# Two-layer hybrid attention trunk on one core: token loads first, the first conditioning in 128-column pieces, late outputs one step later

## The chip, the core and the metric

The kernel runs on one core of a Trainium2 chip. The metric is the device time of one execution in microseconds (us); lower is better. A core has the engines TensorE (PE, matrix products, with its weight loads shown apart as PEld), VectorE (DVE), ScalarE (ACT) and GpSimd (POOL), and SyncE (SP), which here issues transfers. POOL and ACT issue transfers too. All transfers of a core share 16 DMA engines.

## The reference, cut to what matters

128 context tokens (`x_prompt`) and 512 latent tokens (`x_sample`) of width 2048 go through two layers that share weights. Everything is float32.

```python
for layer in range(DEPTH):                       # DEPTH = 2
    sh_p, sc_p, gt_p = modulation(c_ctx, ada_w[layer], ada_b[layer])   # silu(cond) @ w + b, three parts of 2048
    sh_s, sc_s, gt_s = modulation(c, ada_w[layer], ada_b[layer])
    hp = rms_norm(xp, norm_g[layer]) * (1.0 + sc_p) + sh_p
    hs = rms_norm(xs, norm_g[layer]) * (1.0 + sc_s) + sh_s
    ...
        out_p, (kc, vc) = even_mixer(hp, *w)      # layer 0: windowed attention and short gated convolution
        out_s, _ = even_mixer(hs, *w, ctx=(cache_a_k[:, i], cache_a_v[:, i]), rope=rope)
    ...
        out_p, (ckc, cvc, dkc, dvc) = odd_mixer(hp, *w)   # layer 1: differential and grouped-query attention
    ...
    xp = xp + gt_p * out_p
    xs = xs + gt_s * out_s
```

`ada_w` is (2, 2048, 6144) float32. Its columns for one layer are 12 blocks of 512: blocks 0 to 3 give the shift, 4 to 7 the scale, 8 to 11 the gate. One block is 4.19 MB. A mixer starts with one wide projection of the 640 tokens, `h @ w_in`.

## The kernel before

**Layout.** Tokens stand in the free dimension: h is kept as 16 k-tiles (128 of the 2048 features by 640 tokens), each split into a high and a low part, and a weight tile `raw` (up to 4 k-tiles by 128 columns) is split into `wh` and `wl` by ACT and DVE (L241, L242). `proj_q` makes three products for each k-tile and each half of the tokens (320 wide, `pa` and `pb`): wh by high, wh by low, wl by high, at L276 to L278. In the text these are "main matmuls"; one k-tile of one column tile takes six.

**Start.** The conditioning vectors and small parameters are loaded as rows (`rows_a` by SP, `rows_b` by POOL), put through SiLU and transposed (L119 to L127). The tokens come as five blocks of 128 (`x_load`, two pieces of 512 KB each, the first two blocks through ACT's queue, the others through SP's). `x_block` transposes a block on PE in groups of four (L884), copies each group out of PSUM (L885) and sums the squares on ACT (L889); `x_rows` (L899) makes the per-token factor.

**Conditioning on PE.** `ada_on_pe(0, cb, h, n)` multiplies the condition with `n` times 128 columns of block `cb`: 16 small matmuls (L178; the profile shows two passes of each where the profile counts them), a copy, `n` transposes (L184), a reduction, the bias, and for scales the gain. The weights come by SP into two buffers of 2 MB used in turn (`ada_t`), and for block 5 into eight freed token buffers (`spare`, tile name `adah`). The profile's tile `ada` is the first kind.

**Lead phase of layer 0.** h is not there yet when projection starts, so `run_tiles` walks over k first: six column tiles ("leads", four of them summed in SBUF, `sum`) advance together through units of k-tiles. The units before are k 0 to 1, 2 to 3, then 4 to 7, 8 to 11, 12 to 13, 14 to 15 (argument `cut`). Before a unit `h0_maker` makes its h from shift and scale, and `ada_group` (through `ahead`) puts the conditioning of the next unit inside the current one. With four k-tiles to a group, unit 4 to 7 needs blocks 5 and 1. The six weight tiles of a unit are loaded by POOL into four `raw` buffers, except those of the first unit's first four, which SP loads. The order of instructions on each engine is set by a planner of the framework from the order of the code, and is the same in every execution.

**Odd layer.** While PE projects, generators in `attn` (attention) and `prep` (what follows a projected tile) are advanced in slots, four to a column tile; `steps` says how many attention steps a slot gives. `diff_gen` runs one head of the differential attention: scores, softmax, weighting (`weigh`), and `out`, which transposes the weighted result (L1391). The list `brisk` sets 1.1 steps to a slot from job 13 on. In `project_out` a finished output tile is added to the residual (`res_sum`, L1120) and for the second layer transposed to rows and written (`rows_out`, through `to_rows`, L564).

Of the kernel before, what the change touches and what calls it, by code (L numbers as in the profile page):

```python
# [11 lines left out]
F32 = mybir.dt.float32  # L12
# [8 lines left out]
P = 128  # L21
# [21 lines left out]
TRANS = [0, 3, 4, 5]  # L43
GRACE = 3
# [9 lines left out]
def trunk_kernel(ctx: ExitStack, tc: tile.TileContext, I: dict, O: dict):  # L54
# [36 lines left out]
    rows_a = wpool.tile([P, P], F32, tag="raw", name="rows_a")  # L91
# [9 lines left out]
    nc.sync.dma_start(rows_a[0:16, :], I["c"].rearrange("b (k p) -> (b k) p", p=P))  # L101
    nc.sync.dma_start(rows_a[16:32, :], I["c_ctx"].rearrange("(k p) -> k p", p=P))
    nc.sync.dma_start(ident, I["k_ident"])
    nc.sync.dma_start(rows_a[32:64, :], I["norm_g"].rearrange("l (k p) -> (l k) p", p=P))
    nc.sync.dma_start(rows_a[64:112, :], I["ada_b"][0].rearrange("(k p) -> k p", p=P))
    xs = [x_load(b) for b in range(5)]
    rows_b = wpool.tile([P, P], F32, tag="raw", name="rows_b")
# [3 lines left out]
    for i, n in enumerate(("a_q_norm", "c_q_norm", "d_q_norm")):  # L111
# [6 lines left out]
    th = wpool.tile([32, P], F32, tag="raw", name="th")  # L118
    A.activation(th, rows_a[0:32, :], AF.Tanh, scale=0.5)  # L119
    V.scalar_tensor_tensor(out=rows_a[0:32, :], in0=th, scalar=1.0, in1=rows_a[0:32, :],  # L120
                           op0=ALU.add, op1=ALU.mult)
    t0 = psT()
    PE.transpose(t0[:, 0:112], rows_a[0:112, :], ident[0:112, 0:112])
    PE.transpose(t0[:, 128:205], rows_b[0:77, :], ident[0:77, 0:77])
    V.tensor_scalar(sT[:, :, 0:2], t0[:, 0:32].rearrange("p (c k) -> p k c", c=2), 0.5, None, ALU.mult)
    V.tensor_copy(vec[:, 0:80], t0[:, 32:112])
    V.tensor_copy(vec[:, 80:157], t0[:, 128:205])  # L127
# [11 lines left out]
    def ada_done(l, cb, h=0, n=4):  # L139
        fs = slice(cb * 4 + 2 * h, cb * 4 + 2 * h + n)  # L140
        which, k0 = cb // 4, (cb % 4) * 4 + 2 * h
# [11 lines left out]
    def add_bias(l, cb, red, h=0, n=4):  # L153
        fs = slice(cb * 4 + 2 * h, cb * 4 + 2 * h + n)
        V.tensor_tensor(mod[l][:, fs, :], red, ada_b[l][:, fs][:, :, None].to_broadcast([P, n, 2]), op=ALU.add)

    def ada_on_pe(l, cb, h=0, n=4, spare=()):


        acc, m, wd = psT(), 2 if spare else 32 // n, n * P  # L160
        order, ws = list(range(KT)), []
        if spare:
            for i, s in enumerate(spare):
                w = hpool.tile([P, m, wd], F32, tag=f"h{s}", name="adah")
# [746 lines left out]
    for b in range(4):  # L911
        x_block(b, xs[b])
# [717 lines left out]
```

## Time and profile before

| what | value |
|---|---|
| time, median of 3 runs | 2301.63 us (2301.49 to 2303.0) |
| profiled execution | 2303.24 us, of which the span from first to last instruction is 2301.5 us |
| PE busy | 2255.1 us, 98% of the span |
| DVE, ACT, POOL busy | 73%, 43%, 8% of the span |
| mean granted PE clock | 0.997 |
| data moved | 347.52 MB, mean 151 GB/s |

A row of the time line reads: start, duration, engine, line, operation, tile written and tiles read, shape, count; in brackets the time that the engine was idle before it, and what it waited for. A row of the windows table gives for a stretch the busy time of each engine, the granted PE clock, the share of the DMA engines and the rate. Matmuls are pipelined: one of 0.31 us can follow another after 0.15 us.

### The profile page before, as it was taken

To read this page: it belongs to the slowest core of one execution; us is meant where nothing else is said; L and a number is where in the kernel's file an instruction comes from. 1 tells how busy PE (TensorE), PEld (TensorE's weight loads), DVE (VectorE), ACT (ScalarE), POOL (GpSimd) and SP (SyncE) were. 2 spreads that over 40 slices of the span, in tenths; PEclk is the share of its full clock that TensorE was granted. 3 is DMA by queue.
4 is the path that set the end of the run, shared out by engine and by line. 5 is a ranking of instruction groups with operands and counts; after the bars stand their busy time and mean duration, and the time that the engine had idled before them with its cause. 6 is when DMAs were issued, how large, how long until landed. Compare 5 with 4: busy or idle time off the path is not lost.

```text
span 2301.5 us, 41520 instructions
## 1 busy us (share of the span) xinstructions
PE 2255.1 (98%) x15796; PEld 2180.1 (95%) x15796; DVE 1676.7 (73%) x3364; ACT 991.3 (43%) x2043; POOL 182.6 (8%) x251
## 2 busy tenths in 40 slices
PE   7999999999999999999999999999999999999999
PEld 5699999999999999999999999999999999999999
DVE  4559886786877663888787765868868778677676
ACT  4235442433422222544654445455554554554343
POOL 2111000000000000000110000100000111111001
PEclk9999999999999999999999999999999999999999
DMA  9974535435355542954673334413324234237532
GB/s 367 332 257 127 163 117 171 141 113 174 106 179 175 155 140 82 296 150 134 212 240 115 112 119 144 136 58 93 112 74 145 75 114 132 78 106 240 167 120 70
DMA packets 389768, 347.52 MB, mean 151 GB/s; under 512 B 19330, under 2 KB 327056, under 8 KB 389056
## 3 DMA queue, kind: packets, MB, share of 16 engines
q1 hardware_dynamic: 376672, 296.32, 41.9%
q0 software_dynamic: 12176, 46.39, 5.3%
q8 instruction: 124, 2.03, 0.4%
q10 hardware_dynamic: 720, 2.16, 0.3%
q14 instruction: 76, 0.62, 0.1%
HBM read 303.89 MB, written 40.90 MB: 150 GB/s over the span
## 4 chain that ended last, share of the span: by engine, by line
PE 87%; DVE 5%; DMA 3%; ACT 2%; issue 2%; POOL 1%; SPq 0%; POOLq 0%; ACTq 0%; DVEq 0%
PE pa L276 9%; PE pb L276 9%; PE pb L277 9%; PE pa L278 9%; PE pa L277 9%; PE pb L278 9%; PE pq L535 7%; PE pq L537 7%; PE pq L536 7%; PE T L732 2%; PE S L744 1%; PE T L178 1%; PE S L746 1%; PE S L745 1%; PE T L564 1%
## 5 line engine op out<-in xcount | busy, mean ns | idle before, releaser
L241 ACT ACTIVATE wh<-raw 128x512 fp32r<-128x512 f32 (+1 forms) x442 | 273.3, 619 | 664.3 <-PE pb L277 550.3
L276 PE MATMUL pa<-h,wh 128*128 128x320 f32 x1504 | 478.0, 318 | 5.1 <-ACT h L241 2.6
L242 DVE TENSOR_TENSOR wl<-raw,wh 128x512 fp32r<-128x512 f32 (+1 forms) x442 | 297.6, 674 | 238.5 <-ACT wh L241 220.8
L277 PE MATMUL pa<-h,wh 128*128 128x320 f32 x1504 | 467.6, 311 | 1.4 <-DVE h L242 1.4
L278 PE MATMUL pa<-h,wl 128*128 128x320 f32 x1504 | 467.3, 311 | 0.0
L276 PE MATMUL pb<-h,wh 128*128 128x320 f32 x1504 | 466.1, 310 | 0.4 <-DVE xr L1120 0.4
L278 PE MATMUL pb<-h,wl 128*128 128x320 f32 x1504 | 466.3, 310 | 0.0
L277 PE MATMUL pb<-h,wh 128*128 128x320 f32 x1504 | 465.7, 310 | 0.0
L213 DVE SCALAR_TENSOR_TENSOR acc<-adaw,sT,acc 128x512 f32<-128x512 f32 (+1 forms) x600 | 360.3, 639 | 14.3 <-DMA adaw<-in_ada_w 13.8
L276 PEld LDWEIGHTS pa<-h,wh 128*128 128x128 f32 x1504 | 283.3, 189 | 17.6 <-issue 8.9
L277 PEld LDWEIGHTS pa<-h,wh 128*128 128x128 f32 x1504 | 284.1, 189 | 4.5 <-DVE h L242 2.2
L278 PEld LDWEIGHTS pa<-h,wl 128*128 128x128 f32 x1504 | 283.4, 188 | 3.7 <-issue 3.7
L278 PEld LDWEIGHTS pb<-h,wl 128*128 128x128 f32 x1504 | 282.8, 188 | 2.1 <-issue 2.1
L276 PEld LDWEIGHTS pb<-h,wh 128*128 128x128 f32 x1504 | 282.9, 188 | 0.6 <-issue 0.6
L277 PEld LDWEIGHTS pb<-h,wh 128*128 128x128 f32 x1504 | 282.9, 188 | 0.5 <-issue 0.4
L535 PE MATMUL pq<-h,wh 128*128 128x320 f32 x608 | 189.8, 312 | 0.5 <-ACT wh L241 0.5
L536 PE MATMUL pq<-h,wh 128*128 128x320 f32 x608 | 187.9, 309 | 0.0
L537 PE MATMUL pq<-h,wl 128*128 128x320 f32 x608 | 187.7, 309 | 0.0
L718 ACT ACTIVATE p<-S,nm,rq 128x768 f32<-128x768 f32 (+3 forms) x120 | 101.3, 844 | 101.7 <-DVE nm L713 70.1
L535 PE MATMUL pq<-T,wh 128*128 128x320 f32 x456 | 140.9, 309 | 0.0
L536 PE MATMUL pq<-T,wh 128*128 128x320 f32 x456 | 140.9, 309 | 0.0
L537 PE MATMUL pq<-T,wl 128*128 128x320 f32 x456 | 140.9, 309 | 0.0
(339 smaller groups left out, 3933.5 us busy)
## 6 DMA issues: line engine op xcount, KB each, us to landing
adaw<-in_ada_w SPq DMA_DIRECT2D x192, 256.0 KB, 2.9
raw<-in_ev_w_in SPq DMA_DIRECT2D x184, 256.0 KB, 3.0
raw<-in_od_w_in SPq DMA_DIRECT2D x160, 256.0 KB, 2.9
ada<-in_ada_w SPq DMA_DIRECT2D x14, 2048.0 KB, 10.1
adaw<-in_ada_w SPq DMA_DIRECT2D x128, 128.0 KB, 2.1
w<-in_od_w_in SPq DMA_DIRECT2D x24, 512.0 KB, 3.7
yd<-y POOLq DMA_DIRECT2D x32, 320.0 KB, 3.3
w<-yd SPq DMA_DIRECT2D x32, 320.0 KB, 4.1
```

The source lines that it names most:

```text
L178: PE.matmul(acc[32 * g:32 * g + 32, 0:wd], sT[:, kt, :], w[:, kt % m, :], start=(i < 4), stop=(i >= KT - 4), tile_position=(0, 32 * g))
L213: V.scalar_tensor_tensor(out=a, in0=w, scalar=sT[:, kt, c:c + 1], in1=a, op0=ALU.mult, op1=ALU.add)
L241: A.activation(hi, x, AF.Copy)
L242: V.tensor_sub(lo, x, hi)
L276: PE.matmul(ps, wh[:, i, :], hi[:, sl], start=(j == js[0] if alone else (pos == 0 and j == 0)), stop=False)
L277: PE.matmul(ps, wh[:, i, :], lo[:, sl], start=False, stop=False)
L278: PE.matmul(ps, wl[:, i, :], hi[:, sl], start=False, stop=(j == js[1] - 1 if alone else (pos == 3 and j == 3)))
L535: PE.matmul(ps, wh[:, j, :], hi, start=(h == 0 and j == 0), stop=False)
L536: PE.matmul(ps, wh[:, j, :], lo, start=False, stop=False)
L537: PE.matmul(ps, wl[:, j, :], hi, start=False, stop=(h == 1 and j == 3))
L718: A.activation(p[:, 0:n], s, AF.Exp, scale=rsc, bias=nm, accum_out=l)
L732: PE.transpose(t[:, i * P:(i + 1) * P], p, ident)
```

## The change

The five row loads of the conditioning go from SP's queue to POOL's, behind nothing but each other; SP's queue then begins with the identity and the tokens. Token blocks are loaded and transposed in the order 0, 2, 1, 3, 4, and the SiLU of the conditions and its transposes (`cond_in`) come after the fourth of them. `rows_a`, `rows_b` and `th` get places of their own instead of `raw` buffers. ACT copies the last group of a block only for even blocks; DVE copies it for the others.

The first halves of blocks 4 and 0 come as four loads of 128 columns (1 MB each), and the first unit of the lead phase is split in two, k 0 and k 1, so that there are seven units. Four of the eight pieces of block 5 are loaded ahead of the second halves of blocks 4 and 0.

In the odd layer `out` of a head's last block comes one step later, a finished output tile of the last projection is written one slot later, and `brisk` is 1.2 instead of 1.1.

```diff
+ORDER_X = (0, 2, 1, 3, 4)
+SPARE = (15, 14, 11, 10, 13, 12, 9, 8)
-    nc.sync.dma_start(rows_a[0:16, :], I["c"].rearrange("b (k p) -> (b k) p", p=P))
-    nc.sync.dma_start(rows_a[16:32, :], I["c_ctx"].rearrange("(k p) -> k p", p=P))
     nc.sync.dma_start(ident, I["k_ident"])
...
-    xs = [x_load(b) for b in range(5)]
+    xs = {b: x_load(b) for b in ORDER_X}
+    nc.gpsimd.dma_start(rows_a[0:16, :], I["c"].rearrange("b (k p) -> (b k) p", p=P))
...
+    def first_load(cb, j):
+
+        if cb not in first_ws:
+            first_ws[cb] = ada_t[0].rearrange("p (k n) -> p k n", k=KT)
+            ada_t.reverse()
+        c0 = cb * 512 + j * P
+        nc.sync.dma_start(first_ws[cb][:, :, j * P:(j + 1) * P],
+                          I["ada_w"][0, :, c0:c0 + P].rearrange("(k p) n -> p k n", p=P))
...
-            (A.copy if g == 3 else V.tensor_copy)(xT[g][:, :, b * P:(b + 1) * P],
+            (A.copy if g == 3 and b % 2 == 0 else V.tensor_copy)(xT[g][:, :, b * P:(b + 1) * P],
...
-    for b in range(4):
+    for i, b in enumerate(ORDER_X):
         x_block(b, xs[b])
-    ada_on_pe(0, 4, 0, 2)
-    x_block(4, xs[4])
+        if i == 3:
+            cond_in()
+    first_load(4, 0)
+    ada_on_pe(0, 4, 0, 1)
...
-        g = {(4, 0): 0, (4, 4): 1, (5, 0): 2, (5, 4): 3}.get((ui, n))
+        g = {(5, 0): 0, (5, 4): 1, (6, 0): 2, (6, 4): 3}.get((ui, n))
...
+    def first_ada():
+        for cb, j in ((0, 0), (4, 1), (0, 1)):
+            first_load(cb, j)
+        ada_on_pe(0, 0, 0, 1)
+
+        spare_load(0, 5, SPARE[:4])
...
-    run_tiles(jobs, I["ev_w_in"][0], h0_maker, fill0, FILL0, ada_group, trans=TRANS, grace=GRACE, cut=((0, 2), (2, 4)),
-              summed=keep, led=even_start, lead_in=lambda: ada_on_pe(0, 0, 0, 2))
+    run_tiles(jobs, I["ev_w_in"][0], h0_maker, fill0, FILL0, ada_group, trans=TRANS, grace=GRACE, cut={0: ((0, 1), (1, 2), (2, 4)), 3: ((0, 2), (2, 4))},
+              summed=keep, led=even_start, lead_in=first_ada)
...
                     res_sum(l, n, pp[i], CS[:1] if i == 0 else CS[1:])
                 yield
+                if l:
+                    yield
                 finish(n)
...
-            if u < 6:
-                yield
+            yield
             if u >= 2:
                 out(u - 2)
...
-    brisk.update((i, 1.1) for i in range(13, len(jobs)))
+    brisk.update((i, 1.2) for i in range(13, len(jobs)))
```

Two places show how the planner's order moves.

The first is SP's queue at the start. `ada` are pieces of blocks 4, 0 and so on in the two 2 MB buffers, `adah` the pieces of block 5, `raw` weight tiles of the projection. Before, then with the change:

```order
L101 DMA rows_a<-in_c 16x128
L102 DMA rows_a<-in_c_ctx 16x128
L103 DMA ident<-in_k_ident 128x128
L104 DMA rows_a<-in_norm_g 32x128
L105 DMA rows_a<-in_ada_b 48x128
L97 DMA xb<-in_x_sample 128x1024 x4
L97 DMA xb<-in_x_prompt 128x1024 x2
L175 DMA ada_120<-in_ada_w 128x16x256
L254 DMA raw<-in_ev_w_in 128x2x128 x4
L175 DMA ada_121<-in_ada_w 128x16x256
L175 DMA ada_120<-in_ada_w 128x16x256
L175 DMA ada_121<-in_ada_w 128x16x256
L165 DMA adah<-in_ada_w 128x2x512 x8
```

```order
L104 DMA ident<-in_k_ident 128x128
L100 DMA xb<-in_x_sample 128x1024 x4
L100 DMA xb<-in_x_prompt 128x1024 x2
L177 DMA ada_121<-in_ada_w 128x16x128
L277 DMA raw<-in_ev_w_in 128x128 x4
L177 DMA ada_122<-in_ada_w 128x16x128
L177 DMA ada_121<-in_ada_w 128x16x128
L177 DMA ada_122<-in_ada_w 128x16x128
L166 DMA adah<-in_ada_w 128x2x512 x4
L198 DMA ada_121<-in_ada_w 128x16x256
L198 DMA ada_122<-in_ada_w 128x16x256
L166 DMA adah<-in_ada_w 128x2x512 x4
```

The row loads are gone from this queue, two loads of 256 columns have become four of 128, and four pieces of block 5 stand ahead of the last two 256-column loads.

The second is PE around the conditioning of the first group of k-tiles (k 0 to 3, 144 main matmuls) and the start of the second (k 4 to 7). `T<-ada... 32x512 x8` is half of a block, `T<-ident,ada_sb` the transposes behind it, `pa<-h_896` (with the change `pa<-h_995`) the first main matmul of k 4. Before, the end of the first group:

```order
L276 MATMUL pb<-h_694,wh 128x320
L277 MATMUL pb<-h_694,wh 128x320
L278 MATMUL pb<-h_694,wl 128x320
L178 MATMUL T<-ada_121,sT 32x512 x8
L184 MATMUL T<-ident,ada_sb 128x128 x4
L276 MATMUL pa<-h_896,wh 128x320 x2
```

With the change, first the place after 72 main matmuls (k 0 and 1 done), then the place after 123:

```order
L301 MATMUL pb<-h_648,wl 128x320
L201 MATMUL T<-ada_121,sT 32x256 x16
L207 MATMUL T<-ident,ada_sb 128x128 x2
L201 MATMUL T<-ada_122,sT 32x256 x16
L207 MATMUL T<-ident,ada_sb 128x128 x2
L299 MATMUL pa<-h_794,wh 128x320 x2
```

```order
L301 MATMUL pa<-h_794,wl 128x320
L201 MATMUL T<-ada_122,sT 32x512 x8
L299 MATMUL pa<-h_801,wh 128x320
L300 MATMUL pa<-h_801,wh 128x320
L301 MATMUL pa<-h_801,wl 128x320
L299 MATMUL pb<-h_794,wh 128x320
L300 MATMUL pb<-h_794,wh 128x320
L207 MATMUL T<-ident,ada_sb 128x128 x4
```

The last half of block 1 stood behind all 144 main matmuls of the first group; with the change it stands behind 123, and 21 main matmuls lie between it and the second group. The second halves of blocks 4 and 0, which stood among main matmuls, now stand together after the first 72 with none between them and the h that needs them. Behind the lead phase the order on PE is the same up to the middle of the odd layer.

69 lines of the change are left out of this document (38 added, 31 removed).

## The prediction

> **What bounds the kernel now.** I read the page's totals first, then the time line of PE and the windows at the start, then what PE waited for in the odd layer.
>
> ```profile
> span 2301.5 us, 41520 instructions
> PE 2255.1 (98%) x15796; PEld 2180.1 (95%) x15796; DVE 1676.7 (73%) x3364; ACT 991.3 (43%) x2043; POOL 182.6 (8%) x251
> PE   7999999999999999999999999999999999999999
> ```
>
> PE is the bound; it lacks 2301.5 − 2255.1 = 46.4 us over the whole span. Of the 40 slices of the span only the first is below nine tenths busy. The change removes no main matmul, so it can win only idle time and time at a low clock. Here is the start on PE:
>
> ```profile
> 7.86 0.42 PE L123 MATMUL T<-ident,rows_a 112*128 112x112 f32 x1 [7.86 <-DMA rows_a<-in_ada_b]
> 10.93 4.40 PE L884 MATMUL T<-ident,xb 128*128 128x128 f32 x20
> 16.88 4.85 PE L884 MATMUL T<-ident,xb 128*128 128x128 f32 x24 [1.54 <-ACT xT L885]
> 32.91 1.93 PE L178 MATMUL T<-ada,sT 128*32 128x256 f32 x32 [0.45 <-ACT tables L900]
> 37.04 0.56 PE L276 MATMUL pa<-h,wh 128*128 128x320 f32 x2 [1.22 <-ACT h L926]
> 44.21 0.31 PE L276 MATMUL pb<-h,wh 128*128 128x320 f32 x1
> 47.43 0.31 PE L278 MATMUL Sp<-h,wl 128*128 128x320 f32 x1
> 60.88 3.64 PE L178 MATMUL T<-adah,sT 128*32 128x512 f32 x32
> 67.15 1.92 PE L178 MATMUL T<-ada,sT 128*32 128x512 f32 x16
> 71.10 1.92 PE L178 MATMUL T<-ada,sT 128*32 128x512 f32 x16
> 73.78 0.66 PE L184 MATMUL T<-ident,ada_sb 128*128 128x128 f32 x4 [0.76 <-ACT ada_sb L181]
> 75.68 0.90 PE L276 MATMUL pa<-h,wh 128*128 128x320 f32 x2 [1.24 <-ACT h L926]
> ```
>
> ```profile
> 39.00:41.00 2.00, 2.00 (x9) 1.80 (x7) 0.00 (x0) 0.45 (x2) 0.00 (x0) 0.50 1.07 375
> 77.00:79.00 2.00, 2.00 (x9) 2.00 (x8) 2.00 (x5) 0.70 (x2) 0.00 (x0) 0.50 1.03 407
> ```
>
> Two gaps are to be seen: before the first main matmul (37.04) and before the second group of k-tiles (75.68), where the last half of block 1 (71.10) must pass its copy, transposes, bias and h, 0.76 + 1.24 us of idle. The two rows of the windows (the granted clock is the number before the DMA share) show that after each of them PE ran at 0.50 of its clock. The 23 main matmuls from 44.21 to 47.43 come (47.43 − 44.21)/22 = 0.146 us apart. In a stretch of about 3.4 us at half clock, some 1.7 us of work is lost, an estimate from the 0.50 and from the spread of the slow rows between 75.68 and 79.
>
> What stands behind PE there is the transfer of weights:
>
> ```profile
> 0.00:5.00 5.00, 0.00 (x0) 0.00 (x0) 0.59 (x3) 0.00 (x0) 3.39 (x10) 1.00 0.53 179
> 5.00:10.00 5.00, 0.42 (x1) 0.18 (x1) 0.28 (x1) 3.78 (x6) 0.00 (x0) 1.00 0.99 321
> 10.00:20.00 10.00, 7.56 (x37) 5.79 (x37) 5.33 (x15) 5.50 (x11) 1.61 (x3) 0.88 1.03 401
> 20.00:25.00 5.00, 4.55 (x28) 3.08 (x27) 3.88 (x8) 4.56 (x9) 0.61 (x2) 0.90 1.11 373
> 25.00:30.00 5.00, 4.12 (x50) 2.57 (x48) 3.71 (x12) 2.62 (x8) 3.46 (x5) 1.00 1.09 385
> 30.00:45.00 15.00, 12.51 (x113) 9.20 (x111) 6.09 (x17) 5.48 (x13) 0.77 (x2) 0.89 1.07 381
> 45.00:50.00 5.00, 5.00 (x54) 3.88 (x53) 2.47 (x6) 1.55 (x5) 1.44 (x2) 1.00 1.04 397
> 50.00:65.00 15.00, 15.00 (x108) 11.82 (x107) 6.96 (x16) 6.32 (x16) 4.49 (x6) 1.00 1.04 406
> 65.00:70.00 5.00, 5.00 (x40) 3.33 (x39) 4.00 (x11) 1.35 (x3) 0.75 (x1) 1.00 0.73 261
> ```
>
> The DMA engines are full (share above 1) from 10 to 65 us. Multiplying rate by time gives the bytes moved: 2.5 MB at 10 us, 16.0 at 45, 18.0 at 50, 24.1 at 65. So until the second group starts, time is set by bytes as much as by PE.
>
> **The change part by part, the start.** The six-column lead phase needs, up to the last half of block 1: tokens 5.24 MB, small loads 0.14, four blocks of 4.19 (16.8), weight tiles of the first group 6 × 262 KB = 1.6, and the first four tiles of the second group 1.0; in all 24.8 MB. On the table that is 24.1 at 65 us and 0.7 more at 406 GB/s: 66.7 us. The change moves none of these bytes away; the early start of PE (transposes no longer behind the 7.86 us wait for the rows and the ACT copy at 16.88) is therefore worth only what the transfers allow.
>
> What changes in the transfers: SP's queue starts with tokens instead of five small loads. The first 10 us moved 2.5 MB where 401 GB/s would give 4.0; I take 1.0 us of this as won (bounds 0 and 1.5/0.401 = 3.7, the whole hole). The four 128-column loads read 512-byte rows instead of 1 KB. The trace has no window of such rows alone; the 20 to 25 window, with 0.52 MB of them (four tiles of 128 KB), ran at 373 against 381 to 385 around it: 1.34 MB at 0.383 takes 3.5 us, which leaves 1.5 us for 0.52 MB, 350 GB/s. For 4.19 MB that is 12.0 − 10.9 = 1.1 us lost (bounds 0, and 2.6 at 310 GB/s, twice the drop). The two cancel nearly. The Trainium skill, "DMA: Bandwidth & Descriptors", section Specifications, gives 512 bytes as the smallest transfer for line rate; by that the 1.1 us would be nothing and the sum below 1.1 us better.
>
> Now PE. In the new order four pieces of block 5 (2.1 MB) come ahead of the second halves of blocks 4 and 0. The half of block 0 is complete when 5.4 + 8.4 + 2.1 + 1.0 (weight tiles of k 0, 1 and the first of k 2) = 16.9 MB are in, 47.3 us on the table. PE is long through k 0 and 1: main work can begin near 28 us (tokens by about 16.5 us, 20 groups of four transposes at 4.85/6 = 0.8 us each from about 6 us, then two conditioning steps of about 3 us), and 72 × 0.146 = 10.5 us, half blocks 2 × 1.5 and a slow stretch end by 43 to 45. The matmuls of that half start at 47.5, and its chain is that from 32.91 to 37.04, 4.1 us, with a slow clock behind it: k 2 starts at 51.6. From there to the last half of block 1 lie 51 main matmuls (7.4), block 5 (3.64 and 0.45 for transposes), the first half of block 1 (1.92) and the slow clock (1.7): 66.8 us, the same moment as its bytes. I take 68 us for it, since the 261 GB/s row shows the queue running thin with that piece still on its way (bounds 65.5, and 70.5 with the dearer rows). Then 1.92 + 0.45 for its matmuls and transposes and 21 × 0.146 = 3.1 for the main matmuls that now follow it: 73.5 us, and the second group goes on at full clock, its h being made under those 21. Before, the same point was at 75.68 with 1.7 us of slow clock still to pay, in effect 77.4. **The start gains 3.9 us** (bounds: 1.4 with 70.5, and 7 with 65.5 and no slow clock). Behind it PE is the bound again, so the gain stays: no slice after the first is below nine tenths, and 10,692 instructions follow in unchanged order.
>
> ```profile
> L349 DVE TENSOR_TENSOR sum<-sum,pb 128x320 f32<-128x320 f32 x13 | 6.3, 487 | 5.3 <-PE pb L278 5.3
> ```
>
> What is costed at nothing: 32 more conditioning matmuls, at most the 1.93 us of a half block, run while PE waits for block 0; the additions of one more unit, 8 of 0.49 us, and shorter splits lie on DVE, busy 33 of these 70 us (sum of its column above); without that cover, 3.9 us. DVE's copies in blocks 1 and 3 instead of ACT's lie ahead of the first main matmul, where bytes decide. Rows on POOL's queue are ahead of everything that POOL issues; `cond_in`, fourth in line, waits for nothing else. The copies of x to DRAM shift by one unit number with the same matmuls.
>
> **The odd layer.** PE's waits there that the change touches:
>
> ```profile
> 1843.64 0.41 PE L1391 MATMUL T<-ident,on 128*128 128x128 f32 x2 [1.21 <-DVE on L1385]
> 1931.32 0.41 PE L1391 MATMUL T<-ident,on 128*128 128x128 f32 x2 [1.38 <-DVE on L1385]
> 2016.67 0.41 PE L1391 MATMUL T<-ident,on 128*128 128x128 f32 x2 [0.49 <-DVE mod L155]
> 2057.33 0.44 PE L1391 MATMUL T<-ident,on 128*128 128x128 f32 x2 [0.43 <-DVE ptl L242]
> 2124.83 0.41 PE L564 MATMUL T<-ident,xr 128*128 128x128 f32 x2 [0.31 <-issue]
> 2125.51 0.65 PE L564 MATMUL T<-ident,xr 128*128 128x128 f32 x3 [0.27 <-DVE xr L1120]
> 2154.17 0.93 PE L564 MATMUL T<-ident,xr 128*128 128x128 f32 x5 [1.06 <-ACT h L241]
> 1807.56 0.44 PE L744 MATMUL S<-k0h,q0h 128*128 128x384 f32 x1 [0.84 <-ACT p L718]
> 2077.72 0.39 PE L744 MATMUL S<-k1h,q1h 128*128 128x256 f32 x1 [1.07 <-ACT p L718]
> ```
>
> One more step for `out` and for the output tiles aims at 3.5 us (L1391) and 1.6 us (L564), 5.1 in all; some of it will show up at another place, since 16 of the 20 `out` calls are also moved by the new pace; I take 3.9. The pace of 1.2 for 15 jobs of 4 slots gives 60 × 0.1 = 6 more slots with two attention steps, of which 4 go to the four new steps. Two steps in a slot bring two scores close together; the two such waits in the stretch (0.84, 1.07) over its 6 double slots make 0.3 us for each, 1.9 us for six (bounds 0 and 6 × 1.07 = 6.4). **Net gain 2.0 us** (bounds −3.8, with half the gain and every double slot paid, and 5.1).
>
> Sum: 3.9 + 2.0 = 5.9 us from the profiled span, 2295.6. The profiled execution took 2303.24 us, 1.74 around its span, and so becomes 2297.3; it stands 1.6 above the median of the runs, which becomes 2301.63 − 5.9 = **2295.7 us**.
>
> **The rivals.** 0.2% (4.6 us) is about what a measurement of this kernel can tell from no change.
>
> *Bytes take it all.* The dearer rows and the pieces of block 5 in front make the last half of block 1 come at 70.5 or later: start 1.4, odd layer 1.5, time 2298.7. For: a full DMA from 10 to 65 us. Against: the hole before 10 us. Its sister, a price of 1 us for each new double slot, leaves the start's 3.9 and takes 2 to 4 back: 2299.7 to 2301.7.
>
> *The transfers give more.* The hole before 10 us is filled (3.7 us), the second group starts at 70.5 and the odd layer brings 4: 11 us, 2290.6. For: SP's queue held small loads only. Against: two queues already brought tokens from the start.
>
> *Weight tiles starve (slower).* With one k-tile to a unit, a weight tile feeds 6 × 0.146 = 0.88 us of PE, and four `raw` buffers are refilled by POOL:
>
> ```profile
> L254 POOL DMA_DIRECT2D raw<-in_ev_w_in x29: 705/722/779, 27.1 to 139.1; - x29
> DMA to landing us min/median/max: 2.5/5.7/11.5
> ```
>
> A turn of a buffer is 0.72 to issue, 5.7 to land and about 1 to split: 7.4/4 = 1.9 us for a tile, slower than 0.88 but covered by eight tiles loaded or split ahead and by the wait to 47.5. At 11.5 us it would be 13.2/4 = 3.3 us; then the six tiles of k 2 and 3 take 20 us instead of 10.5, the second group starts 9 us later than forecast, 82.7 against 77.4: 5.3 us lost, and 2307 without help from the odd layer. It decides from a turn of 4 × 1.75 = 7 us sustained, above which k 2 and 3 cannot be fed at PE's pace. For: more load in flight; against: the median.
>
> **How the numbers follow.** Forecast 0.47 (2293 to 2297); the transfers give more 0.13; bytes take it all 0.20 and its sister 0.09; starvation 0.11. The range from 2288.5 to 2302 holds the first four but for their tails, about 8 in 10. Faster 0.47 + 0.13 = 0.60, same 0.29, slower 0.11.
>
> **What would show it.** Right: the first main matmul near 28 us; after 72 main matmuls a gap of several us on PE that ends in h and is followed by half clock; no gap of 2 us and no half clock where the second group starts, and that start near 73.5; DMA share near 1 throughout; no wait over 1 us at the transposes of `out` for a head's last block, and some more waits of scores for the softmax. Wrong: the second group later than 76, or a gap inside k 2 and 3 that waits for `wh` or `raw`; forced attention steps in one slot before a new head's keys; more than 4 us of new waits for scores.

## The result and the profile after

The changed kernel took 2308.68 us (median of 8 runs, 2304.71 to 2311.37) where the kernel before took 2301.8 (8 runs, 2299.27 to 2304.27) on the same chip: ratio 1.0023, 95% interval 1.0013 to 1.0032. It is slower, by 5.3 us by the ratio and 6.9 us by the medians; 2295.7, faster, was predicted. Its profiled execution has a span of 2306.9 us, 5.4 more than before's.

First the time line of PE at the start of the changed kernel (start, duration, line, result and operands, and in brackets the idle time ahead and what ended it):

```profile
25.87 1.08 PE L201 MATMUL T<-ada,sT 128*32 128x128 f32 x32 [0.18 <-DVE ssx L915]
32.41 0.56 PE L299 MATMUL pa<-h,wh 128*128 128x320 f32 x2 [0.20 <-ACT h L951]
41.75 0.41 PE L299 MATMUL pb<-h,wh 128*128 128x320 f32 x1 [2.04 <-ACT sum L370]
50.23 0.39 PE L299 MATMUL pa<-h,wh 128*128 128x320 f32 x1 [3.24 <-DVE sum L372]
51.27 3.39 PE L201 MATMUL T<-ada,sT 128*32 128x256 f32 x32
55.50 1.93 PE L201 MATMUL T<-ada,sT 128*32 128x256 f32 x32
59.64 0.56 PE L299 MATMUL pa<-h,wh 128*128 128x320 f32 x2 [1.22 <-ACT h L951]
74.81 1.92 PE L201 MATMUL T<-ada,sT 128*32 128x512 f32 x16
80.34 0.66 PE L299 MATMUL pa<-h,wh 128*128 128x320 f32 x2
```

Then two rows of the windows table (busy us of PE, PEld, DVE, ACT and POOL, the granted clock, DMA share, GB/s):

```profile
52.00:54.00 2.00, 2.00 (x25) 0.92 (x20) 0.21 (x1) 0.00 (x0) 0.84 (x2) 0.50 1.07 418
74.00:82.00 8.00, 8.00 (x56) 5.69 (x55) 4.73 (x11) 4.18 (x8) 1.92 (x3) 1.00 1.04 399
```

The main matmuls start 4.6 us earlier (32.41 against 37.04). Then PE waits 2.04 and 3.24 us inside the first 72 of them, and from 51.27 to 59.64 there is no main matmul at all: the second halves of blocks 4 and 0 are conditioned one behind the other, the first at half clock (the 0.50 from 52 to 54 us). k 2 starts at 59.64 where it started at 54.13 before, and the second group at 80.34 where it was 75.68. At the second group the forecast picture stands: no gap, full clock from 74 to 82. So the change removed the gap it aimed at and made a longer one some 20 us ahead of it. At the 351st main matmul (123.98 us before, 127.90 after) the lag is 3.92 us.

Second, what the two waits are. ACT, which splits the weight tiles, waits for their transfers (same columns). What POOL's loads into the `raw` buffers take is in the view of that tile between 20 and 90 us:

```profile
41.07 0.31 ACT L264 ACTIVATE wh<-raw 128x128 fp32r<-128x128 f32 x1 [2.27 <-DMA raw<-in_ev_w_in]
47.23 0.42 ACT L264 ACTIVATE wh<-raw 128x256 fp32r<-128x256 f32 x1 [2.79 <-DMA raw<-in_ev_w_in]
48.81 0.42 ACT L264 ACTIVATE wh<-raw 128x256 fp32r<-128x256 f32 x1 [1.16 <-DMA raw<-in_ev_w_in]
```

```profile
L277 POOL DMA_DIRECT2D raw<-in_ev_w_in x22: 534/716/756, 23.9 to 82.6; - x22
DMA to landing us min/median/max: 3.9/5.1/6.4
```

PE names the copies `sum` of ACT and DVE as the releasers, but these stand in their engines' order behind a split that waits for a transfer (41.07 for the first wait, 48.81 for the second). It took no slow landing: 5.1 us is the median.

Third, what PE waited for in the odd layer, longest groups first (total, times, longest), before and after:

```profile
PE T L1391 <- DVE on L1385: 2.6, 2, 1.4
PE S L744 <- ACT p L718: 1.9, 2, 1.1
PE T L564 <- DVE m L620: 1.3, 4, 0.6
```

```profile
PE T L587 <- DVE m L643: 3.4, 5, 2.2
...
PE S L767 <- ACT p L741: 0.6, 2, 0.3
```

The waits for `on` are gone, and those for the softmax became smaller, not larger. In their place stands one of 2.2 us for `m`, the rotation of the first key of the second attention.

### The profile page after: what moved, and what is told of

It is laid out like the page before. It is cut to its first block, busy times and chain, and to the rows that moved or that the text cites. A ratio compares the mean times of both kernels' runs of the same rounds, so it can differ in the third digit from the quotient of the medians.

```text
span 2306.9 us, 41700 instructions
## 1 busy us (share of the span) xinstructions
PE 2263.4 (98%) x15860; PEld 2186.2 (95%) x15860; DVE 1682.7 (73%) x3385; ACT 988.7 (43%) x2049; POOL 184.2 (8%) x261
## 4 chain that ended last, share of the span: by engine, by line
PE 87%; DVE 4%; DMA 3%; issue 2%; ACT 2%; POOL 1%; SPq 0%; ACTq 0%; POOLq 0%; DVEq 0%
PE pa L299 9%; PE pb L299 9%; PE pb L300 9%; PE pb L301 8%; PE pa L300 8%; PE pa L301 8%; PE pq L558 7%; PE pq L560 7%; PE pq L559 7%; PE T L755 2%; PE S L767 1%; PE T L201 1%; PE S L769 1%; PE S L768 1%; PE T L587 1%
## 5 line engine op out<-in xcount | busy, mean ns | idle before, releaser
L264 ACT ACTIVATE wh<-raw 128x512 fp32r<-128x512 f32 (+2 forms) x448 | 274.5, 613 | 665.6 <-PE pb L300 544.2
L265 DVE TENSOR_TENSOR wl<-raw,wh 128x512 fp32r<-128x512 f32 (+2 forms) x448 | 298.7, 668 | 214.5 <-ACT wh L264 194.6
```

The costliest lines, as they stand in the source:

```text
L264: A.activation(hi, x, AF.Copy)
L265: V.tensor_sub(lo, x, hi)
```

## The experiments

Fifteen kernels were run. A ratio is the time over that of the kernel before, run beside it, with its 95% interval; 0.1% is 2.3 us. Each row of the table is one trace. The landings of the halves of blocks 4 and 0 are the end of the last packet of that half, counted by row length; that of the last half of block 1 is issue plus time to landing, because the next block's rows have its length. The three starts are those of the first, 73rd and 145th main matmul on PE's time line. Traces of kernels with the same lead phase scatter: the second group starts at 75.0 to 76.3 us with the start of before (four traces), at 73.1 to 74.5 with tokens first (four) and at 79.9 to 80.8 with the changed start (three).

| kernel | ratio, interval | first main | halves of blocks 4, 0 landed | k 2 | last half of block 1 landed | second group |
|---|---|---|---|---|---|---|
| before | 1 | 37.0 | 36.5, 42.8 | 54.1 | 69.1 | 75.7 |
| changed | 1.0023, 1.0013–1.0032 | 32.4 | 41.5, 48.8 | 59.6 | 69.6 | 80.3 |
| start alone | 1.0030, 1.0019–1.0040 | 33.2 | 42.7, 50.4 | 59.2 | 70.4 | 79.9 |
| weight tiles in own places | 1.0020, 1.0010–1.0030 | 32.8 | 44.0, 51.8 | 58.0 | 68.9 | 78.7 |
| no early pieces | 1.0039, 1.0027–1.0052 | 33.0 | 40.1, 47.7 | 56.9 | 72.9 | 80.1 |
| pieces between the halves | 1.0029, 1.0018–1.0040 | 32.4 | 40.7, 51.8 | 56.4 | 70.2 | 78.2 |
| the same, tiles in own places | 1.0037, 1.0023–1.0051 | 32.8 | 41.5, 51.1 | 57.8 | 68.5 | 81.0 |
| quarter in own place, no pieces | 1.0055, 1.0043–1.0068 | 32.3 | 36.7, 44.8 | 55.7 | 70.2 | 85.5 |
| the same, two k-tiles to a unit | 1.0030, 1.0019–1.0040 | 33.0 | 37.0, 43.6 | 51.7 | 70.2 | 80.0 |
| tokens first alone | 0.9996, 0.9987–1.0005 | 35.1 | 36.7, 43.4 | 50.7 | 69.9 | 74.5 |

**The three odd-layer edits alone.** The kernel before with

```
+                if l:
+                    yield
...
-            if u < 6:
-                yield
+            yield
...
-    brisk.update((i, 1.1) for i in range(13, len(jobs)))
+    brisk.update((i, 1.2) for i in range(13, len(jobs)))
```

> The kernel before with only the three odd-layer edits. Theory (the loss of the changed kernel sits in the lead phase, up to main matmul 350; the odd layer gives a little back): about 1 us faster than before, 2300.8 (2299.5 to 2302), no wait over 0.5 us at the transposes of out, start rows as before. My forecast's term says 2.0 us faster, 2299.8. Rival (the double slots of the pace cost more than the waits they remove, and this is why the changed kernel is slower): 2 to 4 us slower, 2304 to 2306, with several new waits of scores for the softmax.

Measured: 2305.14 against 2304.68, ratio 1.0000 (0.9991 to 1.0009): no change that can be told. The interval is 2.1 us to either side, so the rival's 2 to 4 us of loss are out but for their edge, and the theory's 1 us of gain is not decided. The waits of PE in the odd layer changed places:

```profile
PE T L564 <- DVE m L620: 5.3, 5, 3.5
```

No wait for `on` is left, and the one for `m` takes back 3.5 us. Its cause is on DVE's time line and in SP's queue. First the kernel before:

```profile
1767.19 0.69 DVE L600 TENSOR_TENSOR kg<-T,gain_rows 128x512 f32<-128x512 f32 x1 [0.83 <-ACT junk L598]
1768.95 0.48 DVE L213 SCALAR_TENSOR_TENSOR acc<-adaw,sT,acc 128x256 f32<-128x256 f32 x1 [0.79 <-DMA adaw<-in_ada_w]
```

```profile
1758.17 0.41 SPq L207 DMA_DIRECT2D adaw<-in_ada_w  x1
1763.24 0.82 SPq L1483 DMA_DIRECT2D y<-gd  x2
1764.63 2.08 SPq L207 DMA_DIRECT2D adaw<-in_ada_w  x3
```

Then this one:

```profile
1770.66 0.48 DVE L213 SCALAR_TENSOR_TENSOR acc<-adaw,sT,acc 128x256 f32<-128x256 f32 x1 [3.50 <-DMA adaw<-in_ada_w]
1771.06 0.68 DVE L600 TENSOR_TENSOR kg<-T,gain_rows 128x512 f32<-128x512 f32 x1
1776.50 0.68 DVE L620 TENSOR_TENSOR m<-m,m 128x512 f32<-128x512 f32 x1
```

```profile
1764.73 1.88 SPq L1484 DMA_DIRECT2D y<-gd  x2
1767.14 1.45 SPq L207 DMA_DIRECT2D adaw<-in_ada_w  x3
```

In both kernels three adaw loads stand behind the two gate copies `y<-gd`. Two things differ. Before, one more adaw load had gone out at 1758.17, ahead of the copies; now the next ones go out at 1767.14. And before, `kg` stood on DVE ahead of the step that waits for adaw; now this step, with its wait of 3.50 us, stands ahead of `kg` and so of `m`, which need no adaw, and PE stands behind `m`.

**The start alone.** The changed kernel with these three edits undone. The next seven kernels also have the odd layer of before.

> The changed kernel with the three odd-layer edits undone: its start alone. Theory: k 2 starts near 59.6 us and the second group near 80.3 as in the changed kernel, and the whole is 4 to 8 us slower than before, 2306 to 2310 (3.9 from the lead, and up to 3 where the transfers later meet a wait). Rival (the odd layer is the loss): the start alone is equal or faster, 2298 to 2302, whatever the lead phase shows.

Measured: 2311.07 against 2304.68, 1.0030 (1.0019 to 1.0040). The theory held, with k 2 at 59.2 and the second group at 79.9: the loss is in the start.

**Tokens first alone.** The start with block halves of 256 columns, two k-tiles to a unit and block 5 late, as before the change:

```
-    first_load(4, 0)
-    ada_on_pe(0, 4, 0, 1)
+    ada_on_pe(0, 4, 0, 2)
...
     def first_ada():
-        for cb, j in ((0, 0), (4, 1), (0, 1)):
-            first_load(cb, j)
-        ada_on_pe(0, 0, 0, 1)
-        spare_load(0, 5, SPARE[:4])
+        ada_on_pe(0, 0, 0, 2)
...
-    cut={0: ((0, 1), (1, 2), (2, 4)), 3: ((0, 2), (2, 4))}
+    cut={0: ((0, 2), (2, 4)), 3: ((0, 2), (2, 4))}
```

> Tokens first and rows on POOL's queue, but blocks 4 and 0 in halves of 256 columns, units of two k-tiles and block 5 loaded late, as before; odd layer as before. Theory (the fine units starve and the two quarter conditionings stand uncovered; the tokens' order is harmless): first main matmul 1 to 3 us earlier than 37.04, second group start 73 to 76, the time 0 to 3 us faster than before, 2298.8 to 2301.8. Rival (the new order of tokens and the small loads on POOL's queue are what delays): first main matmul not earlier and second group after 76, time 2303 or more.

Measured: 0.9996 (0.9987 to 1.0005), no change that can be told, with first main matmul and second group inside the theory's bounds. The 3.4 us won by k 2 shrink to 1.2 at the second group, because PE there waits for bytes (this kernel's time line):

```profile
69.89 1.92 PE L201 MATMUL T<-ada,sT 128*32 128x512 f32 x16 [1.62 <-DMA ada<-in_ada_w]
72.58 0.66 PE L207 MATMUL T<-ident,ada_sb 128*128 128x128 f32 x4 [0.76 <-ACT ada_sb L204]
74.47 0.89 PE L299 MATMUL pa<-h,wh 128*128 128x320 f32 x2 [1.24 <-ACT h L950]
```

In the three other traces with this start (the kernels below that add odd-layer edits to it) k 2 starts at 50.05 to 51.96 and the second group at 73.1 to 73.5; in all four the group starts 4.6 to 4.8 us after the last half of block 1 has landed. What is left of the start's loss is the finer conditioning, the finer units and the early pieces.

**Weight tiles in places of their own.** The start alone, with

```
-        raw = wpool.tile([P, js[1] - js[0], P], F32, tag="raw", name="raw")
+        if js[1] - js[0] == 1:
+            raw = sp.tile([P, 1, P], F32, tag="raw1", name="raw1", bufs=12)
+        else:
+            raw = wpool.tile([P, js[1] - js[0], P], F32, tag="raw", name="raw")
```

> The start of the changed kernel with twelve weight tiles of the first two k-tiles in places of their own, so that no load of them waits for a split; odd layer as before. Theory (weight tiles starve): the waits for raw behind the splits of the first 72 main matmuls go, these end by about 46 us instead of 51, but the conditioning of blocks 4 and 0 still stands uncovered from about 49 on; second group start 76 to 79 instead of 80.3, the time 1.5 to 4 us less than the start alone. Rival (the bytes set the moment of the second group): second group start stays within 1 us of 80.3 and the time within 1 us of the start alone.

Measured: 2308.83, 2.2 us below the start alone, 1.0020 (1.0010 to 1.0030). The long waits inside the first 72 are gone, the 72nd starts at 46.51 instead of 52.04. The theory's figures came out, the second group at 78.7 and the time 2.2 us lower, though the intervals of the two kernels overlap. But k 2 starts only 1.2 us earlier than in the start alone, and the second group too: with the tiles' bytes ahead of it, the half of block 0 landed at 51.8 instead of 50.4, and PE waited 2.85 us for it. So starvation is real and by itself small.

**No early pieces.** The line `spare_load(0, 5, SPARE[:4])` taken out of the start alone.

> The start alone without the four early pieces of block 5: the second halves of blocks 4 and 0 come 2.1 MB (5.2 us at 400 GB/s) earlier, and block 5 after them. Theory (two causes in line: the pieces make the halves late, and both halves' conditioning stands on PE with no main matmul beside it): the first 72 main matmuls still meet the waits behind the raw transfers, but k 2 starts by 53 to 55 instead of 59.2; the last half of block 1 is then met uncovered again, the second group starts at 75 to 77, 3 to 5 us less than the start alone, time 2305 to 2308 where before is 2304.7. Rival (starvation by units of one k-tile alone): k 2 within 1.5 us of the start alone, time as the start alone, 2310 to 2312.

Measured: 2312.2 against 2302.83, 1.0039 (1.0027 to 1.0052). Both fall: the theory on k 2 (56.9, not 53 to 55), the second group (80.1, not 75 to 77) and the time, the rival on k 2, which came 2.3 us earlier than in the start alone. The half of block 0 landed only 2.7 us earlier, not 5.2. The windows from 30 to 35 us, of the kernel before, of the changed kernel and of this one, say why (the last two numbers are DMA share and GB/s):

```profile
30.00:35.00 5.00, 4.11 (x49) 2.54 (x46) 2.75 (x6) 1.38 (x4) 0.05 (x1) 1.00 1.07 387
```

```profile
30.00:35.00 5.00, 4.36 (x91) 3.36 (x83) 3.06 (x11) 2.39 (x7) 0.00 (x0) 1.00 1.05 401
```

```profile
30.00:35.00 5.00, 4.36 (x89) 3.50 (x92) 3.07 (x10) 2.24 (x7) 0.00 (x0) 1.00 0.55 185
```

Without the pieces the DMA stands half idle. The early pieces fill a hole, and the hole was what I had not seen. SP's issue of block 4's second half before, and then in the changed kernel, where also what SP waited for up to 70 us is shown (in all, times, longest):

```profile
27.44 0.37 SPq L175 DMA_DIRECT2D ada<-in_ada_w  x1
```

```profile
32.27 0.37 SPq L198 DMA_DIRECT2D ada<-in_ada_w  x1
```

```profile
SPq L198 <- PE T L201: 15.1, 3, 9.5
```

There are two buffers of 16 KB for each partition. Before, block 4's first half was read in one step, from 25.45 to 27.38 on PE's time line, and its buffer was free. Now the buffer holds two quarters, and the second is read third in line, from 31.13 to 32.21: the request goes out 4.8 us later (32.27 − 27.44).

**The pieces between the halves**, and the same with the weight tiles' own places: `spare_load` moved behind the load of block 4's half, which puts that conditioning on PE after main matmul 51 instead of 72.

> The start alone with the four early pieces of block 5 issued between the two halves, behind that of block 4: the bytes ahead of the half of block 0 stay the same, and on PE only the conditioning of block 4 moves, from main matmul 72 to 51. Theory (the pair that stands together costs the time of one conditioning, 2.8 us): k 2 starts 2.5 to 4 us earlier than in the start alone, 55 to 57, and the second group 2.5 to 4 us earlier, 76 to 77.5; time 2306 to 2309. Rival (bytes of the last half of block 1 decide the second group): k 2 earlier, the second group not before 79, time within 1 us of the start alone.

> The same placing of the pieces, and the twelve weight tiles of the first two k-tiles in places of their own. Theory (nothing but the landing of block 0's half is left, and that was at 48.8 us in the changed kernel): k 2 at 53 to 56, the second group at 74 to 76.5, time 2303 to 2306. Rival (weight tiles that are no longer held back by buffers take their bytes ahead of the half, as in the run with places alone, where it landed near 52.4): k 2 at 57 or later, the second group at 78 or later, time 2308.

Measured: k 2 at 56.4, 2.8 us earlier than the start alone, and the second group 1.7 earlier, less than the 2.5 to 4 expected; the whole 1.0029, not to be told from the start alone. So the two conditionings that stand together cost at k 2 the 2.8 us of the theory, and less than that further on. With own places for the tiles the rival came true: half of block 0 at 51.1, k 2 at 57.8, second group at 81.0.

**The quarter in a place of its own.** The start without pieces, block 4's second quarter in 8 KB more, so that the buffer is free after the first step; then also with two k-tiles to a unit:

```
+    quarter = pre.tile([P, KT, P], F32, name="quarter")
...
-        nc.sync.dma_start(first_ws[cb][:, :, j * P:(j + 1) * P],
+        w = quarter if (cb, j) == (4, 1) else first_ws[cb][:, :, j * P:(j + 1) * P]
+        nc.sync.dma_start(w,
...
-                w = first_ws[cb][:, :, j0 * P:(j0 + 1) * P]
+                w = quarter if (cb, j0) == (4, 1) else first_ws[cb][:, :, j0 * P:(j0 + 1) * P]
```

> The start without the four early pieces, and the second quarter of block 4 in a place of its own (8 KB for each partition), so that the buffer in which block 4's first and second quarter lay is read out earlier and its second half can be asked for earlier; units of one k-tile and 128-column loads stay. Theory (the second halves are late because both buffers are held by quarters until the third conditioning step, and the early pieces only fill that hole): the half of block 4 is issued near 28 us instead of 32.9 and lands at 36 to 39, that of block 0 at 42 to 45 instead of 47.7; k 2 starts at 51 to 54 with no conditioning of its own ahead of it; second group 73 to 77; 3 to 7 us less than the run without pieces, within 2 us of before. Rival (the 512-byte rows and the one-k units cost this by themselves): block 0's half stays behind 46 us or k 2 behind 55, and the time within 1.5 us of the run without pieces.

> The same, with the first two k-tiles in one unit of 128 KB weight tiles as before the change; only the loads of 128 columns are left of the finer start. Theory (of what is left after the buffer, the waits for raw at one k-tile to a unit cost about 1 us): no wait of 2 us inside the first 72 main matmuls, k 2 at 50 to 53, time 0 to 2 us less than with one-k units and 0 to 2 us less than before. Rival (one-k units cost nothing once the halves come early): the same time as with one-k units within 0.5 us, the same k 2 within 0.5 us.

Measured: the buffer theory holds for the transfers. The half of block 4 is issued at 26.93 and lands at 36.7, that of block 0 lands at 44.8; k 2 at 55.7 with units of one k-tile, 1.7 us later than the theory's 54 and beyond the rival's 55, and 51.7 with units of two, so finer units do cost about 4 us there once the halves are early. Both miss on the time, 1.0055 and 1.0030: a new wait took the place, of 4.94 us in the first. The time line of the second:

```profile
70.24 1.92 PE L202 MATMUL T<-ada,sT 128*32 128x512 f32 x16 [1.58 <-DMA ada<-in_ada_w]
72.92 0.66 PE L208 MATMUL T<-ident,ada_sb 128*128 128x128 f32 x4 [0.76 <-ACT ada_sb L205]
78.17 1.88 PE L202 MATMUL T<-ada,sT 128*32 128x512 f32 x2 [4.59 <-DMA ada<-in_ada_w]
```

In the new order the next block's first conditioning matmuls stand on PE ahead of the second group, and their 2 MB piece lands 4.59 us after PE is ready. Without that the group would have started 1.9 us after the transposes at 72.92, as in the rows of tokens first (72.58 to 74.47): 74.8, an estimate. In no run did the last half of block 1 land before 68.4 us.

**Tokens first and the odd-layer edits.**

> Tokens first with halves of 256 columns, together with the odd-layer edits. Theory (the two are independent, lead 1.2 us and odd layer about 1 us in their profiles): 1 to 2.5 us faster than before; second group start near 74.5. Rival (both gains are within what a measurement can tell, or are lost to later waits for transfers): within 0.1% of before either way.

Measured: 2303.51 against 2302.83, 1.0000 (0.9992 to 1.0009): the rival, though the theory's 1 us still lies in the interval.

**Steps and pace apart**, each put alone into the kernel before: the two `yield` edits with pace 1.1, and the pace of 1.2 without them.

> The kernel before with the two added steps alone (a step more in the projection of the odd layer's outputs and in the making of an output tile), the pace left at 1.1. In the run with all three edits the waits for on went (2.6 us in two) and a wait of 3.5 us for m came, at the first head of the second attention, behind an adaw transfer that DVE waited 3.50 us for. Theory (the faster pace moves adaw's issue behind the copies y<-gd in SP's queue and makes the wait for m): without it the wait for m stays under 1.2 us, the waits for on still go, and the time is 1 to 2.5 us less than before. Rival (the steps themselves shift the queue): the wait for m is 2 us or more as in the run with all three, and the time within 1 us of before.

> The kernel before with the pace of 1.2 alone, without the added steps. Theory (the pace makes the wait for m): a wait for m of 2 us or more behind adaw near 1775 us, the waits for on stay at 1.2 and 1.4, the time 1 to 4 us more than before. Rival (the pace is harmless, the steps make it): the wait for m below 1.2 us, the time within 1 us of before.

Measured: the steps alone 2301.43 against 2303.94, 0.9989 (0.9980 to 0.9998); the pace alone 2308.59, 1.0019 (1.0010 to 1.0028). The longest wait for `m`, steps and then pace:

```profile
PE T L564 <- DVE m L620: 2.7, 4, 1.8
PE T L1393 <- DVE on L1387: 2.1, 2, 1.4
```

```profile
PE T L564 <- DVE m L620: 4.6, 5, 3.1
PE T L1391 <- DVE on L1385: 1.4, 1, 1.4
...
PE S L744 <- ACT p L718: 0.6, 2, 0.3
```

The steps win 2.5 us and the pace loses 4.7 (2308.59 − 2303.94) alone, both on the theory's side. In detail both missed: with the steps the wait for `m` is 1.8, neither under 1.2 nor over 2, and both waits for `on` are still there, 1.4 and 0.7; with the pace one of them is gone, and it needs steps and pace to remove both. The pace's own wait is the 3.1 us for `m`. On DVE's time line of the pace alone, the step that waits for adaw stands ahead of `kg`, as in the kernel with all three edits:

```profile
1771.39 0.48 DVE L213 SCALAR_TENSOR_TENSOR acc<-adaw,sT,acc 128x256 f32<-128x256 f32 x1 [3.12 <-DMA adaw<-in_ada_w]
```

With the steps alone it waits 2.37 us but stands behind `kg`, as in the kernel before. So the order comes with the pace. That this wait is where the pace's 4.7 us start is read from the traces; no kernel moved the adaw loads alone.

**Pace 1.1 in the changed kernel, and the parts that help put together**: the changed kernel with pace 1.1; tokens first with the steps, at pace 1.1 and at 1.0.

> The changed kernel with the pace put back to 1.1, everything else as changed. Theory (parts add up: start +6.4 us, steps -2.5, pace +4.4 alone): 2 to 5 us less than the changed kernel, 2304 to 2308 where before is 2302 to 2304, so still slower than before by 1 to 5; the lead phase as in the changed kernel. Rival (the pace costs nothing once the start has shifted the phase of the transfers, as its wait for m of 2.2 us against 3.1 to 3.5 hints): the same as the changed kernel within 1 us, 5 to 7 us above before.

> Tokens first with halves of 256 columns and block 5 late, the two added steps, the pace at 1.1. Theory (the parts add up, 0.5 and 2.5 us): 2 to 4 us less than before, 2299 to 2301 where before is 2303. Rival (tokens first gives nothing, or what it wins in the lead is lost at later waits for adaw): the same as the steps alone, 2.5 us less than before or fewer.

> The same with the pace at 1.0, no double slots in the second attention. Theory (each double slot costs about 0.7 us, 4.4 us for six by the run with the pace alone): another 2 to 4 us less, 2296 to 2299. Rival (without double slots the last attention steps come late and the tail waits for them): 2 us or more above the run at 1.1, with new waits for on or xr in the last 250 us.

Measured against 2304.09: the changed kernel at pace 1.1 2309.66, 1.0022 (1.0013 to 1.0030), the rival: the pace's loss is not there in the changed kernel, or is below what the intervals let one see (0.1%). Tokens first with the steps took 2299.56, 0.9980 (0.9971 to 0.9988), 4.5 us less than before: **this one beats both kernels**. The parts alone make 3.0 (0.5 and 2.5), which lies inside its interval of 2.8 to 6.7 us (0.12% and 0.29%); that they add up is not contradicted, and no more than that. At pace 1.0 it is 2301.74, 0.9990 (0.9981 to 0.9998), with a wait for `m` of 2.4 again; 2.2 us more than at 1.1, which is the rival's time. The expected gain was not there, and so the cost of a double slot is no fixed price.

## Why the prediction was wrong, point by point

**Start gain of 3.9 us: wrong in sign.** The profiles show a loss of 3.9 us by main matmul 351. The failing step is "k 2 starts at 51.6", which came at 59.64, and it has three parts.

- "PE is long through k 0 and 1 … end by 43 to 45." The first main matmul came at 32.41, not 28. The conditioning took what was forecast (25.87 to 32.41, against two steps of about 3 us); the transposes of the tokens ahead of it ended at 25.69, not near 22. Their last ten groups took 0.8 us each, as forecast (18.02 to 25.69), but the first ten took 1.3 (4.95 to 17.84), with waits of 1.63 us for tokens and of 0.79 and 0.78 for DVE's copies. And the 72nd main matmul started at 51.04, because the turn of four `raw` buffers was *not* "covered by eight tiles loaded or split ahead" once a tile fed 0.88 us only. The prediction had this as the starvation rival and tied it to a landing of 11.5 us. By its own figures the median was enough: a turn of 7.4 us, above the 7 us that it named as the limit for k 2 and 3, let alone for tiles of 0.88 us. The median landing that came, 5.1 us, did it.
- "The matmuls of that half start at 47.5, and its chain is that from 32.91 to 37.04, 4.1 us". The bytes were nearly right: block 0's half landed at 48.8 against 47.3 to 47.5 forecast. But PE takes its instructions in order, and behind the 72nd main matmul the half of block 4 stands first: 51.27 to 55.50 with its slow clock, and only then block 0's step and the 4.1 us from 55.50 to 59.64. The order of PE that the document shows ahead of the prediction had both steps together there; I costed one. The 8.0 us between 51.6 and 59.64 are thus 3.8 of late start (47.5 to 51.27) and 4.2 of the step that had no term.
- The early pieces were counted as 2.1 MB ahead of the half, which they are. Not seen was that without them the queue would have run dry, since quarters hold both buffers. Removing any one of these (own tile places, pieces elsewhere, no pieces) won only 1 to 3 us at k 2, as the next in line then decided; freeing the buffer, without early pieces and with units of two k-tiles, won 7.5 (59.21 to 51.72).

**The price of the second gap.** The forecast counted 1.7 us of half clock behind the gap at 75.68 as lost in every execution of the kernel before. Its profile has this stretch. But the kernels with only odd-layer edits have the same lead phase and the same gap, 0.76 and 1.24 us, and two of the three traces show no half clock there. The windows of before, and of the three odd-layer edits alone:

```profile
75.00:80.00 5.00, 4.32 (x20) 4.01 (x24) 4.34 (x9) 3.48 (x7) 0.00 (x0) 0.66 1.04 405
```

```profile
75.00:80.00 5.00, 3.81 (x25) 2.73 (x26) 4.18 (x10) 3.11 (x7) 0.00 (x0) 1.00 1.04 408
```

The second of them starts its second group 0.5 us later and still reaches the 351st main matmul at 123.05 us, 0.9 earlier than before's trace. So a good part of the aim is there in some executions and not in others, and the lag of the changed kernel at that point is 3.9 to 4.9 us, by the trace that one takes.

**The last half of block 1: right.** It landed at 69.6 us against 68, inside the bounds, with no gap and full clock at the second group. In the changed kernel it did not decide: PE came to it only at 74.81. With PE early enough, as in tokens first, it does, and the second group starts at 73.1 to 74.5, 1.2 to 2.6 us before the old time. That is near the 1.4 us of the rival *Bytes take it all*, and it is why there was little to win. (The upper bound of the start's gain, 7 us, comes to 77.4 − 71.0 = 6.4 by the prediction's own terms.)

**512-byte rows.** I took 350 GB/s, 1.1 us for 4.19 MB. From 18 to 26 us the changed kernel (by its transfer records, rows of 512 bytes alone) and tokens first alone (1 KB, but for 0.52 MB) moved:

```profile
18.00:22.00 4.00, 3.64 (x24) 2.51 (x24) 3.84 (x9) 3.94 (x9) 0.55 (x1) 1.00 1.10 328
22.00:26.00 4.00, 3.37 (x24) 2.08 (x26) 3.85 (x15) 4.00 (x10) 1.19 (x3) 1.00 1.12 336
```

```profile
18.00:22.00 4.00, 3.81 (x21) 2.66 (x20) 3.56 (x8) 3.91 (x8) 0.53 (x1) 1.00 1.09 384
22.00:26.00 4.00, 3.39 (x22) 2.25 (x22) 3.65 (x13) 3.94 (x8) 0.78 (x3) 1.00 1.11 373
```

At a full DMA that is 332 against 378.5, an eighth less; for 4.19 MB 12.6 against 11.1 us, 1.5 us. Over all traces it is 317 to 344 with loads of 128 columns (nine) and 378 to 379 with 256 (eight), 1.1 to 2.1 us. The term was sized about right, at the low end. The Trainium skill's rule quoted in the prediction ("DMA: Bandwidth & Descriptors", Specifications: 512 bytes are enough for line rate) does not fit this stretch.

**Odd layer, net gain of 2.0 us: 0.0 alone, with 2.1 us of interval to either side.** The steps were taken at 3.9 and measured 2.5. The pace was taken at 1.9, through collisions of scores in double slots; it measured 4.7 alone, inside the bound of 6.4 but by another way: the waits for the softmax shrank to 0.6, and the loss sits at one adaw tile for which DVE stops. The order of the adaw steps on DVE, and of their loads in SP's queue, had no term in my sum.

**The starvation rival, at 0.11, had the right sign and nearly the time** (2307 against 2308.7). The time is luck: it put 5.3 us on weight tiles in k 2 and 3, which did not wait, and the waits that came, in k 0 and 1, are worth 1.2 of the 4.2 us that the start alone loses at the second group.

**What stays open.** Between main matmul 351 and the end the start-alone profile loses 3.7 us more (3.45 to 7.1 behind before's span), the changed one 1.5 (3.92 to 5.4). Both lags stay as they are up to the 600th main matmul (3.46 and 3.93) and are 4.97 and 6.05 at the 700th. Between them lies DVE's wait for the first adaw tile after the lead phase; PE's wait for the `kg` that DVE makes behind it is 1.06 us before, 3.03 in the changed kernel and 2.43 in the start alone. DVE before and after:

```profile
172.25 0.88 DVE L211 TENSOR_SCALAR acc<-adaw,sT 128x512 f32<-128x512 f32 x2 [5.22 <-DMA adaw<-in_ada_w]
```

```profile
178.15 0.88 DVE L234 TENSOR_SCALAR acc<-adaw,sT 128x512 f32<-128x512 f32 x2 [7.19 <-DMA adaw<-in_ada_w]
```

It was not tried by itself. At the 8,600th main matmul (1701 us before) the lags are 4.25 and 6.30; the rest, 2.9 us more in the start alone and 0.9 us less in the changed kernel, comes in the odd layer and is not explained. Nor was a start tried with freed buffer whose order keeps the next block's matmuls behind the second group. Why the pace costs nothing in the changed kernel is open too.

## What to carry to other kernels

When a load is cut finer to start earlier, ask which buffer the pieces hold and until when: the next load of that buffer is late by the time of the last piece's reader, and a gap in the queue appears where none was. When a stall of PE is forecast, read in PE's own order everything that stands behind the blocked instruction, and count each chain; and if the bytes ahead of a point are unchanged, the point moves at most to its bytes. Look at more than one trace before a stretch at low clock is counted as a gain: here two traces of four with the same lead phase had none. Measure the parts of a change apart: here two of four helped or cost nothing, and those alone made 2299.6 us of 2304.1.

## What the runs showed of the hardware

Rows of 512 bytes lowered the rate of a full DMA by an eighth, 328 to 336 against 373 to 384 GB/s in the pair above; a packet of 512 bytes took 27 ns in the mean there, one of 1 KB 46 ns. And a stretch at half clock comes in other places than forecast, so that what stands right behind a wait can pay for it: 32 conditioning matmuls took 3.39 us instead of 1.93 at 51.27 in the changed kernel, 1.0 us after its wait of 3.24. Its wait of 2.04 us at 41.75 brought none: the clock of the windows behind the two waits is

```profile
42.00:47.00 5.00, 4.97 (x31) 4.30 (x30) 2.82 (x8) 1.53 (x5) 2.86 (x4) 1.00 1.08 390
51.00:55.00 4.00, 3.66 (x35) 1.44 (x33) 1.21 (x4) 0.71 (x2) 1.50 (x2) 0.57 1.05 393
```

The length of the wait alone does not decide: at the same main matmul, the changed kernel at pace 1.1 waited 2.07 us and was granted 0.57 from 42 to 46 us, and the gap of 0.76 and 1.24 us before the second group brought half clock in some traces and not in others of the same lead phase. What decides, the runs don't show.
